# The front of a hybrid flow step: w_in as plain fp32 products, the S5 tables, splits and taps on VectorE alone, and the first modulation from row slabs

## The chip, the cores and the metric

The kernel runs on one core of one Trainium2 chip. The metric is the device time of one execution in microseconds; lower is better. TensorE is PE, VectorE DVE, ScalarE ACT, GpSimd POOL and SyncE SP in what follows.

## The reference, cut to what matters

One layer works on two groups of 128 tokens each (a context and a latent grid) with shared weights, D = 1024:

```python
mod = silu(cond) @ w_mod + b_mod            # per group; six parts of 1024: sh1, sc1, g1, sh2, sc2, g2
h = rmsnorm(x, norm1_g) * (1 + sc1) + sh1
z = h @ w_in + b_in                         # (256 tokens, 5120 columns)
z_f, z_a, z_b, z_s, z_g = split(z)          # 512 Fourier, 512 + 512 conv, 512 S5, 3 x 1024 gates
br_f = fft2(z_f).real @ w_four
br_c = silu(layernorm(depthwise_conv31(z_a * sigmoid(z_b)))) @ w_conv_out
y_s, finals = s5_bidirectional(z_s, ...)    # complex diagonal scan, 32 groups of 16 channels, 64 states
y_s = gelu(y_s) * sigmoid(gelu(y_s) @ w_ssm_glu + b)
br_s = y_s @ w_ssm_out
x = x + g1 * ((gate_f * br_f + gate_c * br_c + gate_s * br_s) @ w_out)
h = rmsnorm(x, norm2_g) * (1 + sc2) + sh2
x = x + g2 * moe(h)                         # 32 experts, top 4, clamped SwiGLU, d_ff 1024
return rmsnorm(x), finals
```

All is fp32. Weights are 1 MB slabs of fp32: 24 of w_mod, 20 of w_in, two for each of three branch projections, four of w_out, and then the experts'.

## The kernel before, in words

The program has a front (modulation, norm, w_in, the three branches, w_out, the router) and then the loop over the experts that tokens chose. The front is not written in engine order. Some thirty generators, one for each part of the work, yield operations; the class `Sched` plans them when the program is built: it keeps a planned time for every engine, adds a cost for each operation from the helpers (`tr` L262, `mm` L273, `ts` L279 and L282, `stt` L287, `tt` L291, `act` and `copy` L304, `vcopy` L311, `fill` L318), and takes next what can start earliest, weighted by the priorities in `PRIO`. So a changed cost or priority changes the order on every engine. On the chip each engine follows its own list, with semaphores between them.

Weights go through `Ring`: slabs are loaded over SP's queue in a fixed order into slots of 8 KB per partition, 23 in all, each as a slot falls free (`ring.done`, `ring.give`). The experts' slabs follow the front's in the same ring.

The parts that matter here:

- `first_mod` and `modulate` (L486 to L545): the first two parts of the modulation, 2048 columns, from eight slabs of w_mod. Before, a slab holds 256 columns of all 1024 rows, so four pieces become ready one after the other; each goes through a copy (`R0`), four transposes, a sum, an addition and a multiplication into `modA`, and then 4 of 16 blocks of the normed, transposed input `xT` are modulated.
- `splitter` and `main_products`: each slab of w_in, of a projection and of w_out is split into two fp32r parts, high (ACT copies 512 columns) and low (DVE or POOL subtracts); `faster` picks the engine by the planned times and the costs `CV`, `CG`. `prod3` then makes a product of three fp32r matmuls of 128x256. The modulated input is split the same way into `hhi` and `hlo`. `COLS` is the order of w_in's slabs ahead of the first projection: S5 columns (1536, 1792), Fourier columns (0, 256), then the conv's.
- S5: `s5_inputs` and `tables_in` make the input tables (four blocks, each of six 128x1024 operations in `cprod`), one generator on DVE and one on POOL, which share a list of blocks. `m1_transposes` turns them for PE. The scan is 16 steps of four 128x128 DVE operations. `tables_out` makes the output tables in the same way as `tables_in`. `kernel_table` makes the table Kd with small matmuls, writes it to DRAM and reads it back in another layout over SP's queue; the matmuls on it (called M3 here) and the S5 output gate follow.
- `taps_sum` makes the 31 taps of the conv for four blocks of 128 channels: three blocks as DVE operations of L287, the last (`NP` = 1) as ACT multiplications and POOL additions.
- `evacuate` takes w_in's and the projections' products out of PSUM and adds the gated branches (`mac`).

Of the kernel before, what the change touches and what calls it, by code (L numbers as in the profile page):

```python
# [205 lines left out]
def build(tc, A, O):  # L206
# [3 lines left out]
    with es:  # L210
# [216 lines left out]
        dma("Y", mrow[0:16], A["b_mod"][0, 0:2048].rearrange("(k p) -> k p", p=128))  # L427
        dma("Y", mrow[16:24], A["norm1_g"][0].rearrange("(k p) -> k p", p=128))
# [32 lines left out]
        R0 = [SL[15][:, 1024:1536], SL[15][:, 1536:2048]]  # L461
        modA = sm.tile([128, 2, 8, 2], F32, name="modA")
        pm = sm.tile([128, 4, 2], F32, name="pm")
        hhi = new(4, F32R)[:, :].rearrange("p (k t) -> p k t", k=8)
        hlo = new(5, F32R)[:, :].rearrange("p (k t) -> p k t", k=8)
# [31 lines left out]
        def first_mod():  # L497
# [19 lines left out]
        def modulate():  # L517

            for b in range(4):
                yield f"R{b}"  # L520
                if b == 0:
                    yield tr(PB[2][:, 64:96], mrow)
                    yield copy(vec[:, 60:84], PB[2][:, 64:88])
                for i in range(4):
                    yield tr(PB[2][:, i * 128:(i + 1) * 128], R0[b % 2][:, i * 128:(i + 1) * 128])
                flags.add(f"P{b}")
                k2 = slice(2 * b, 2 * b + 2)
                yield vsum(pm[:, :, :], PB[2][:, :].rearrange("p (i q r) -> p i r q", i=4, q=4)[:, :, 0:2])
                yield tt(modA[:, :, k2], pm[:, :, :].rearrange("p (s k) g -> p s k g", s=2), vec[:, 60:76].rearrange("p (s k) -> p s k", s=2)[:, :, k2, None].to_broadcast(
                    [128, 2, 2, 2]), OP.add)  # L530
                yield stt(modA[:, 1, k2], modA[:, 1, k2], 1.0, vec[:, 76 + 2 * b:78 + 2 * b, None].to_broadcast([128, 2, 2]),
                          op0=OP.add, op1=OP.mult)
# [8 lines left out]
                if b == 3:  # L541
                    yield tr(PB[2][:, 0:64], vrow)
                    yield copy(vec[:, 0:60], PB[2][:, 0:60])
                    flags.add("vec")
# [132 lines left out]
        def s5_inputs():  # L677
# [23 lines left out]
            yield tt(tb[2], Bt[:, 1], bch(fr), e="G")  # L701
            yield tt(tb[1], Bt[:, 1], bch(fi))
            yield tt(tb[3], Bt[:, 0], bch(fi), e="G")
            yield tt(Bb[:, 0], tb[0], tb[1], OP.subtract)
            yield tt(Bb[:, 1], tb[2], tb[3], OP.add, e="G")
# [59 lines left out]
        def faster(n, cv, cg):  # L765

            return "V" if sch.t["V"] + n * cv <= sch.t["G"] + n * cg else "G"
# [13 lines left out]
        Mtmp = [tbuf(SL16[:, 1024:2048]), tbuf(SL[11][:, 1024:2048])]  # L781

        def cprod(o_re, o_im, tmp, P, Q, Qi, j, e):
# [8 lines left out]
            yield tt(o_re, px(0), qx(Q[0]), e=e)  # L792
            yield tt(tmp, px(1), qx(Q[1]), e=e)
            yield tt(o_re, o_re, tmp, OP.subtract, e=e)
            yield tt(o_im, px(0), qx(Q[1] if Qi is None else Qi), e=e)
            yield tt(tmp, px(1), qx(Q[0]), e=e)
            yield tt(o_im, o_im, tmp, OP.add if Qi is None else OP.subtract, e=e)
# [5 lines left out]
        def tables_in(e, tmp, js):  # L803
            yield from need("Bb", "pw0")
            while js:
                j = js.pop(0)
                yield from cprod(*M1T[j], tmp, pw1, (Bb[:, 0], Bb[:, 1]), None, j, e)
                flags.add(f"T{j}")

        def m1_transposes(js, banks):  # L810
            yield from need("xT", "R2", *(("m0",) if js[0] else ()))
            for j in js:
                if j == 2:
                    yield "in0"
# [10 lines left out]
        def tables_out(e, tmp, js):  # L825
            yield from need("E", "columns", "pw1")
            while js:
                j = js.pop(0)
                yield from cprod(M2[j][:, :, 0], M2[j][:, :, 1], tmp, pw2, (Ct[:, 0], Ct[:, 1]), nCi, j, e)
# [50 lines left out]
        def s5():  # L880
# [100 lines left out]
            for o in range(4):  # L981
# [3 lines left out]
                yield from split(g2[:, c], m_[:, c], m_[:, 1024 + 256 * o:1280 + 256 * o], e="V")  # L985
# [3 lines left out]
        def taps_sum(j):  # L989
# [3 lines left out]
            for k in range(31):  # L993
                if j >= 4 - NP:
                    o = 1536 + 256 * (k % 2 if NP == 1 else j % 2)
                    o = av if k == 0 else SL17[:, o:o + 256].rearrange("p (b t) -> p b t", b=2)
# [4 lines left out]
                elif k == 0:  # L1001
# [5 lines left out]
        def conv():  # L1007
# [23 lines left out]
            for i in range(2):  # L1031
                c = slice(512 * i, 512 * i + 512)
                yield from split(HA[:, c], m_[:, c], m_[:, 1024 + 512 * i:1536 + 512 * i], e="V")
# [718 lines left out]
NP = 1  # L1752
# [22 lines left out]
```

## Time and profile before

| | us |
|---|---|
| median of 3 runs | 1414.85 (1414.38 to 1416.57) |
| profiled execution: its own time | 1418.22 |
| its span, first to last instruction | 1416.4 |
| PE busy (weight loads apart) | 1243.9 |
| DVE busy | 492.4 |
| ACT busy | 301.5 |
| POOL busy | 216.0 |
| mean granted PE clock | 0.961 |

The span is 1.8 us shorter than the execution's own time. The page's shares are averages over a front of some 385 us and an expert part of some 1015 us, which have different limits, so times have to be read by stage. The stages used below are cut at: the first S5 input table on DVE (29.4), the first w_in product (66.8), the first scan operation (107.1), the end of the scan (167.4), the start of Kd's writes (186.7), the first matmul on the Kd read back (219.8), the end of the S5 branch (255), the conv branch's first projection (317.5), the last w_out product (372.8), and the first expert matmul (385.1).

### The profile page before, as it was taken

The page shows a single profiled execution, that of the slowest core. Times are in us where ns is not written, and L with a number is a line of the kernel's source. Part 1 is how long each engine was busy: PE and PEld are TensorE (multiplying, and loading weights), DVE is VectorE, ACT ScalarE, POOL GpSimd, SP SyncE. Part 2 cuts the span into 40 slices and gives each one's busy share as a digit, 9 for nine tenths or more (in the row PEclk, how much of TensorE's full clock was granted, in tenths as well). Part 3 has the DMA queues.
Part 4 walks back from the last instruction along what each step waited for, and adds up shares of the span by engine and source line. Part 5 has one row for each costly group of instructions (what it writes and reads, how often), then busy time and mean ns, then how long its engine had stood idle before and what let it go on. Part 6 is the DMA issues. An engine that isn't in the chain of part 4 may idle for free. (4 is left out here: it accounts for less than half of the span.)

```text
span 1416.4 us, 19588 instructions
## 1 busy us (share of the span) xinstructions
PE 1243.9 (88%) x7444; PEld 655.7 (46%) x7444; DVE 492.4 (35%) x839; ACT 301.5 (21%) x609; POOL 216.0 (15%) x183
## 2 busy tenths in 40 slices
PE   4596787899999999999989999999999989999994
PEld 3475686789833433334343433333334334343331
DVE  7949898897511111111111111111121111211113
ACT  4454344454311101011100101101011101111011
POOL 4555556565300000000000000000000000000001
PEclk9798899999999999999999999999999999999996
DMA  9563489558799999999998999998999994999990
GB/s 268 193 210 115 144 146 266 188 196 316 290 352 410 416 397 415 416 416 415 417 415 319 407 417 414 415 400 357 416 416 416 416 409 185 413 415 415 414 395 33
DMA packets 124834, 477.08 MB, mean 337 GB/s; under 512 B 11871, under 2 KB 49505, under 8 KB 90864
## 3 DMA queue, kind: packets, MB, share of 16 engines
q1 hardware_dynamic: 121744, 468.25, 85.3%
q0 software_dynamic: 2288, 5.76, 1.2%
q8 instruction: 120, 1.97, 0.6%
q10 hardware_dynamic: 624, 0.63, 0.1%
q14 instruction: 58, 0.48, 0.1%
HBM read 472.61 MB, written 1.61 MB: 335 GB/s over the span
## 5 line engine op out<-in xcount | busy, mean ns | idle before, releaser
L273 PE MATMUL pb<-sl,sl 128*64 128x512 f32 (+4 forms) x5344 | 951.3, 485 | 48.7 <-PEq L1644 13.1
L273 PEld LDWEIGHTS pb<-sl,sl 128*64 128x64 f32 (+2 forms) x5344 | 438.4, 152 | 521.8 <-issue 445.2
L304 ACT ACTIVATE sl<-sl 128x512 fp32r<-128x512 f32 (+4 forms) x211 | 120.8, 588 | 614.2 <-DVE sl L279 496.4
L291 POOL TENSOR_TENSOR sl<-sl,sl 128x512 fp32r<-128x512 f32 (+4 forms) x73 | 121.1, 1667 | 737.5 <-DVE sl L291 607.7
L279 DVE TENSOR_SCALAR sl<-pb 128x512 f32<-128x512 f32 (+1 forms) x35 | 23.7, 676 | 434.7 <-PE pb L273 434.7
L287 DVE SCALAR_TENSOR_TENSOR sl<-pb,wsl,sl 128x512 fp32r<-128x512 f32 x64 | 47.7, 750 | 310.5 <-ACT sl L304 309.3
L291 DVE TENSOR_TENSOR sl<-sl,sl 128x512 fp32r<-128x512 f32 (+3 forms) x107 | 105.6, 1001 | 30.1 <-ACT sl L304 27.7
L304 ACT ACTIVATE sl<-pb 128x512 f32<-128x512 f32 (+6 forms) x125 | 68.5, 585 | 199.2 <-PE pb L273 177.8
L262 PE MATMUL pb<-cst,sl 128*128 128x128 f32 (+2 forms) x354 | 57.4, 296 | 46.0 <-ACT sl L304 15.0
L304 ACT ACTIVATE sl<-pb,wsl 128x512 fp32r<-128x512 f32 x64 | 43.6, 687 | 199.6 <-PE pb L273 196.6
L273 PE MATMUL pb<-sl,PT 128*128 128x512 f32 x256 | 78.0, 428 | 0.5 <-PEq L1644 0.5
L273 PE MATMUL pb<-hb,sl 128*128 128x128 f32 x512 | 68.4, 289 | 7.9 <-DVE hb L291 7.5
L273 PEld LDWEIGHTS pb<-hb,sl 128*128 128x128 f32 x512 | 65.1, 200 | 18.3 <-ACT wsl L304 11.8
L262 PEld LDWEIGHTS pb<-cst,sl 128*128 128x128 f32 (+2 forms) x354 | 43.7, 158 | 63.0 <-issue 26.1
L318 POOL MEMSET sl<- 128x30 f32 (+6 forms) x15 | 2.8, 228 | 374.1 <-PEq L1644 373.8
L287 DVE SCALAR_TENSOR_TENSOR hb<-sl,taps,hb 128x256 f32<-128x256 f32 x90 | 55.5, 664 | 0.6
L273 PEld LDWEIGHTS pb<-sl,PT 128*128 128x128 f32 x256 | 46.2, 201 | 8.0 <-ACT sl L304 1.3
L291 POOL TENSOR_TENSOR sl<-PWT,sl 128x1024 f32<-128x1024 f32 x20 | 43.5, 2190 | 11.1 <-PE pb L273 6.2
L273 PEld LDWEIGHTS pb<-comb,hb 128*128 128x128 f32 x128 | 19.6, 207 | 44.6 <-DVE sl L279 41.9
L291 DVE TENSOR_TENSOR sl<-sl 128x512 f32<-128x512 f32 (+4 forms) x77 | 37.1, 500 | 4.1 <-ACT sl L304 0.5
L273 PE MATMUL pb<-comb,hb 128*128 128x1 f32 x128 | 22.0, 241 | 18.2 <-PEq L1644 16.4
L273 PE MATMUL pb<-ha,selb 128*64 128x512 bf16 (+1 forms) x140 | 21.3, 390 | 16.8 <-PEq L1644 14.4
(176 smaller groups left out, 547.0 us busy)
## 6 DMA issues: line engine op xcount, KB each, us to landing
sl<-w_gate_up SPq DMA_DIRECT2D x256, 1024.0 KB, 14.9
sl<-w_down SPq DMA_DIRECT2D x128, 1024.0 KB, 17.5
sl<-w_mod SPq DMA_DIRECT2D x24, 1024.0 KB, 7.2
sl<-w_in SPq DMA_DIRECT2D x20, 1024.0 KB, 11.1
sl<-w_out SPq DMA_DIRECT2D x4, 1024.0 KB, 6.9
sl<-md POOLq DMA_DIRECT2D x6, 512.0 KB, 6.9
sl<-w_four SPq DMA_DIRECT2D x2, 1024.0 KB
sl<-Kd SPq DMA_DIRECT2D x16, 128.0 KB, 9.2
```

Of the source, the lines that this page charges most:

```text
L262: return sch.op("P", 0.107 * in_.shape[0] / 128, [out], [in_], lambda: te.transpose(out, in_, ident[:in_.shape[0], :in_.shape[0]]))
L273: lambda: te.matmul(out, lhsT, rhs, start=start, stop=stop, skip_group_check=True))
L279: return sch.op(e, c, [o], ap, lambda: ENG[e].tensor_scalar(o, a, s1, None, op0=op0))
L287: lambda: ENG[e].scalar_tensor_tensor(o, a, sc, b, op0=op0, op1=op1))
L291: return sch.op(e, c, [o], [a, b], lambda: ENG[e].tensor_tensor(o, a, b, op=op))
L304: [a] + [x for x in (bias, scale) if hasattr(x, "tensor")], lambda: s.activation(o, a, func, **kw))
L318: return sch.op(e, size(o) * 0.9e-3 + 0.1, [o], [], lambda: ENG[e].memset(o, val))
```

## The change

- w_in's products are plain fp32: 16 matmuls of 128x256 per slab on the slab as loaded and on `xT`, which `modulate` overwrites in place (ACT for one group, DVE for the other). Only the projections' and w_out's slabs are split, all by ACT and DVE. `hhi`, `hlo`, `UNITS`, `faster`, `CV` and `CG` go.
- POOL makes no tables, no splits, no tap additions and no additions of gated branches; all four tap blocks and both kinds of table are on DVE.
- The first modulation reads eight slabs of 128 whole rows, 2048 columns each; `adaln`, the function for the later slabs, makes four 32x512 matmuls of each, and `modA` is made once for all.
- The biases of the modulation and the norm's gain are loaded over POOL's queue instead of SP's, the S5 input matrices over ACT's. All first slots are given at once.
- `COLS` has the Fourier columns first. The gated sums lie in slot 5 instead of 20, and those slots are given back at other points. The planner's cost of an fp32r matmul is 4.6e-4 us per column instead of 4.17e-4.

```diff
@@ mm
-                c = max(n, m) * 4.17e-4
+                c = max(n, m) * 4.6e-4
@@ ring
-        for k in range(4):
-            if k == 3:
-                add_cols(("in", COLS[0]), A["w_in"][0], COLS[0], 256, 8)
-            for i in range(2):
-                add_cols(("m0", k, i), A["w_mod"][0], 1024 * i + 256 * k, 256, 8)
+        for k in range(8):
+            ring.add(("m0", k), lambda sl: sl[:, :], A["w_mod"][0, k * 128:(k + 1) * 128, 0:2048])
+        add_cols(("in", COLS[0]), A["w_in"][0], COLS[0], 256, 8)
@@ loads
-        dma("Y", mrow[0:16], A["b_mod"][0, 0:2048].rearrange("(k p) -> k p", p=128))
-        dma("Y", mrow[16:24], A["norm1_g"][0].rearrange("(k p) -> k p", p=128))
-            dma("Y", BR[i].rearrange("g d p h -> g d (p h)"), A[n][0].rearrange("d g p h -> g d (p h)"))
-        start(0, 1)
-        start(2, 3)
-        start(6, 7, 8, 9)
+            dma("S", BR[i].rearrange("g d p h -> g d (p h)"), A[n][0].rearrange("d g p h -> g d (p h)"))
+        start(0, 1, 2, 3, 6, 7, 8, 9, 4)
+        dma("G", mrow[0:16], A["b_mod"][0, 0:2048].rearrange("(k p) -> k p", p=128))
+        dma("G", mrow[16:24], A["norm1_g"][0].rearrange("(k p) -> k p", p=128))
@@ first_mod
-            for b in range(4):
-                for i in range(2):
-                    w = ring.get(("m0", b, i))[:, :].rearrange("p (k c) -> p k c", k=8)
-                    for k in range(8):
-                        q = 32 * (k % 4)
-                        yield mm(PB[b % 2][q:q + 32, 256 * i:256 * i + 256], cs[:, k, :], w[:, k], k < 4 and i == 0, k >= 4)
-                    ring.done(("m0", b, i))
-                if b > 1:
-                    yield f"P{b - 2}"
-                yield copy(R0[b % 2], PB[b % 2][:, :])
-                flags.add(f"R{b}")
+            for k in range(8):
+                yield from adaln(("m0", k), PB[0])
+                if k == 4:
+                    flags.add("R0")
@@ modulate
+            yield "m0"
+            yield copy(R0, PB[0][:, :])
+            for i in range(4):
+                yield tr(PB[2][:, i * 128:(i + 1) * 128], R0[:, i * 128:(i + 1) * 128])
...
             for b in range(4):
-                yield f"R{b}"
...
                 yield f"xT{b}"
                 for k in (2 * b, 2 * b + 1):
                     for g in range(2):
-                        yield act(hhi[:, k, 128 * g:128 * g + 128], xT[:, k, g], AF.Identity, bias=modA[:, 0, k, g:g + 1],
-                                  scale=modA[:, 1, k, g:g + 1])
-                        yield ts(xT[:, k, g], xT[:, k, g], modA[:, 1, k, g:g + 1], modA[:, 0, k, g:g + 1])
-                    yield tt(hlo[:, k], flat(xT[:, k]), fv(hhi[:, k]), OP.subtract)
+                        if g:
+                            yield ts(xT[:, k, g], xT[:, k, g], modA[:, 1, k, g:g + 1], modA[:, 0, k, g:g + 1])
+                        else:
+                            yield act(xT[:, k, g], xT[:, k, g], AF.Identity, bias=modA[:, 0, k, g:g + 1], scale=modA[:, 1, k, g:g + 1])
@@ split
-        def split(src, hi, lo, e=None):
+        def split(src, hi, lo):
             yield copy(hi, src)
-            yield tt(lo, src, fv(hi), OP.subtract, e=e or faster(size(src), CV, CG))
+            yield tt(lo, src, fv(hi), OP.subtract)
@@ taps_sum
-                if j >= 4 - NP:
...
-                    yield act(o, vp[:, j, :, k:k + 128], AF.Identity, scale=taps[:, j, k:k + 1],
-                              **({"bias": vec[:, 40 + j:41 + j]} if k == 0 else {}))
-                    if k:
-                        yield tt(av, av, o, OP.add, e="G")
@@ main_products
+                if key[0] == "in":
...
+                    for n, (k, c) in enumerate((x, c) for x in range(8) for c in range(2)):
+                        if key == seq[0] and c == 0:
+                            yield f"hmod{k}"
+                        yield mm(bk[:, c * 256:(c + 1) * 256], w[:, k, c * 128:(c + 1) * 128], flat(xT[:, k]), n == 0, k == 7)
@@ generators
-                         ("in", tables_in("V", Mtmp[0], js[0])), ("in", tables_in("G", Mtmp[1], js[0])),
+                         ("in", tables_in(Mtmp)),
-                         ("out", tables_out("V", Mtmp[0], js[1])), ("out", tables_out("G", Mtmp[1], js[1])),
+                         ("out", tables_out(Mtmp)),
@@ constants
-COLS = (1536, 1792, 0, 256, 1024, 1280, 512, 768)
+COLS = (0, 256, 1536, 1792, 1024, 1280, 512, 768)
```

The order of the instructions moves on every engine. On DVE, the end of the scan before (`sl_847` is the scan's state, `A8r` and `A8i` its factors, `sl_396<-..,sl_395` a low part of w_in, `PWT` a table product, `sl_1116` a low part of the Fourier branch):

```order
L291 TENSOR_TENSOR sl_847<-sl_847,w_156 128x128
L291 TENSOR_TENSOR sl_396<-sl_69,sl_395 128x512
L291 TENSOR_TENSOR sl_847<-sl_847,w_156 128x128
L291 TENSOR_TENSOR sl_74<-sl_74,sl_84 128x8x128
L291 TENSOR_TENSOR sl_74<-PWT,sl_80 128x8x128
L291 TENSOR_TENSOR sl_84<-PWT,sl_80 128x1024
L291 TENSOR_TENSOR w_156<-A8i,sl_847 128x128
L291 TENSOR_TENSOR w_156<-A8r,sl_847 128x128
L291 TENSOR_TENSOR sl_396<-sl_70,sl_395 128x512
L291 TENSOR_TENSOR sl_847<-sl_847,w_156 128x128 x2
```

and the same place in the change (`sl_754` is the scan's state, `fin` its end, `sl_85` the conv's input vp):

```order
L291 TENSOR_TENSOR w_154<-A8i,sl_754 128x128
L291 TENSOR_TENSOR w_154<-A8r,sl_754 128x128
L291 TENSOR_TENSOR sl_754<-sl_754,w_154 128x128 x2
L311 COPY fin<-sl_754 128x8x4 x2
L291 TENSOR_TENSOR sl_74<-sl_74,sl_84 128x8x128
L291 TENSOR_TENSOR sl_74<-PWT,sl_80 128x8x128
L291 TENSOR_TENSOR sl_84<-PWT,sl_80 128x1024
L287 SCALAR_TENSOR_TENSOR sl_85<-pb_93,vec,ha 128x2x128 x2
L291 TENSOR_TENSOR sl_74<-sl_74,sl_84 128x8x128
L291 TENSOR_TENSOR sl_75<-PWT,sl_80 128x8x128
```

The scan's steps stand next to each other now, and the output tables behind them, all of them on DVE.

On DVE at the start of the change (`sl_79` holds the input factors, `cs` the condition, `sl_87` is `xT`):

```order
L291 TENSOR_TENSOR cs<-pb_95,csg 128x2x8
L291 TENSOR_TENSOR sl_85<-PWT,sl_79 128x1024
...
L291 TENSOR_TENSOR sl_84<-sl_84 128x1024
L291 TENSOR_TENSOR sl_78<-PWT,sl_79 128x1024
L291 TENSOR_TENSOR modA<-pb_95,vec 128x16
L287 SCALAR_TENSOR_TENSOR modA<-modA,vec 128x16
L291 TENSOR_TENSOR modA<-pb_95,vec 128x16
L282 TENSOR_SCALAR sl_87<-sl_87,modA 128x128 x6
```

Twelve table operations stand between `cs` and the three for `modA`; before, four sets of small `modA` operations were spread over the tables.

On PE, the first product of w_in before (`sl_147` and `sl_148` are the parts of a slab, `sl_395` and `sl_396` those of the input):

```order
L273 MATMUL pb_94<-sl_68,cs 32x256 x8
L262 MATMUL pb_96<-cst,sl_83 128x128
L262 MATMUL pb_96<-cst,sl_84 128x128
L262 MATMUL pb_95<-cst,sl_83 128x128 x4
...
L273 MATMUL pb_93<-sl_147,sl_395 128x256
L273 MATMUL pb_93<-sl_148,sl_395 128x256
L273 MATMUL pb_93<-sl_147,sl_396 128x256
```

and in the change (`sl_72` is the slab itself):

```order
L273 MATMUL pb_93<-sl_76,cs 32x512 x4
L477 MATMUL pb_100<-ones 64x64
L273 MATMUL pb_93<-sl_77,cs 32x512 x4
L262 MATMUL pb_96<-cst,sl_85 128x128 x4
...
L262 MATMUL pb_98<-cst,sl_85 128x128 x4
L273 MATMUL pb_93<-sl_87,sl_72 128x256 x4
L273 MATMUL pb_95<-sl_68,cs 32x512 x4
```

The eight w_mod slabs stand ahead of all transposes of tables but a few, and one matmul stands where three did.

## Rows read from the trace of the kernel before

**Rows 1.** Stages: bounds, length, busy of PE, PEld, DVE, ACT, POOL, clock, DMA share, GB/s.

```profile
29.40:66.70 37.30, 23.05 (x185) 13.54 (x186) 36.71 (x43) 17.15 (x39) 25.88 (x19) 0.82 0.73 240
...
107.10:167.40 60.30, 37.51 (x245) 31.91 (x244) 58.09 (x80) 26.49 (x59) 38.06 (x19) 0.79 0.31 109
...
255.00:317.50 62.50, 55.49 (x432) 53.64 (x433) 55.53 (x74) 30.75 (x57) 39.11 (x37) 0.95 0.51 171
317.50:372.80 55.30, 52.87 (x417) 51.31 (x416) 35.34 (x42) 26.12 (x55) 29.34 (x26) 0.97 0.84 312
...
385.10:1400.00 1014.90, 937.83 (x4718) 387.97 (x4717) 164.23 (x278) 120.86 (x239) 3.11 (x6) 0.98 0.96 388
```

**Rows 2.** Timeline of DVE: start, length, engine, line, operation, count [idle before <-what ended it].

```profile
58.57 2.72 DVE L291 TENSOR_TENSOR sl<-sl,sl 128x512 fp32r<-128x512 f32 x1
...
61.48 1.22 DVE L291 TENSOR_TENSOR sl<-PWT,sl 128x1024 f32<-128x1024 f32 x1
...
107.31 0.68 DVE L291 TENSOR_TENSOR sl<-sl,sl 128x512 fp32r<-128x512 f32 x1
...
111.59 0.29 DVE L291 TENSOR_TENSOR w<-A8i,sl 128x128 f32<-128x128 f32 x1
...
112.65 0.29 DVE L291 TENSOR_TENSOR w<-A8i,sl 128x128 f32<-128x128 f32 x1
...
123.29 4.42 DVE L291 TENSOR_TENSOR sl<-sl,w 128x128 f32<-128x128 f32 x2
...
216.98 2.45 DVE L287 SCALAR_TENSOR_TENSOR hb<-sl,taps,hb 128x256 f32<-128x256 f32 x6
```

**Rows 3.** Timeline of POOL beside the first of them.

```profile
58.34 2.40 POOL L291 TENSOR_TENSOR sl<-sl,sl 128x1024 f32<-128x1024 f32 x1
```

**Rows 4.** DVE's groups, 0 to 385.1: line, operation, shapes, count, busy, mean ns, idle before.

```profile
L291 DVE TENSOR_TENSOR sl<-sl,sl 128x512 fp32r<-128x512 f32 x74 | 74.9, 1022 | 26.0 <-ACT sl L304 25.5
L287 DVE SCALAR_TENSOR_TENSOR hb<-sl,taps,hb 128x256 f32<-128x256 f32 x90 | 55.5, 664 | 0.6
L291 DVE TENSOR_TENSOR sl<-sl,w 128x128 f32<-128x128 f32 x32 | 23.4, 730 | 0.4
L291 DVE TENSOR_TENSOR sl<-PWT,sl 128x1024 f32<-128x1024 f32 x12 | 19.5, 1647 | 5.4 <-PE pb L273 5.4
```

**Rows 5.** PE windows: fp32 and fp32r products (busy, clock, DMA); one timeline row.

```profile
238.19:245.20 7.01, 7.01 (x33) 1.00 1.08 362
172.29:179.18 6.89, 6.89 (x60) 1.00 1.03 361
...
103.51 6.97 PE L273 MATMUL pb<-sl,sl 128*128 128x256 f32 x56
```

**Rows 6.** Timeline of PE and ACT: first w_in product, S5 columns out, kernel table, its reader.

```profile
66.79 3.12 PE L273 MATMUL pb<-sl,sl 128*128 128x256 f32 x13
...
89.53 0.84 ACT L304 ACTIVATE sl<-pb,vec 128x256 f32<-128x256 f32 x2 [0.48 <-PE pb L273]
...
179.65 0.40 PE L273 MATMUL pb<-sl,sl 128*32 128x16 f32 x5
...
219.82 0.64 PE L273 MATMUL pb<-sl,sl 128*32 128x128 f32 x4 [5.28 <-DMA sl<-Kd]
```

**Rows 7.** Timeline of SP's queue.

```profile
6.24 19.65 SPq L256 DMA_DIRECT2D sl<-w_mod  x6
...
186.71 9.55 SPq L256 DMA_DIRECT2D Kd<-sl  x16
...
324.81 24.50 SPq L256 DMA_DIRECT2D sl<-w_gate_up  x8
```

**Rows 8.** List of waits, 0 to 385.1: total us, times, longest.

```profile
PE pb L273 <- ACT sl L304: 17.5, 7, 11.9
PE pb L273 <- DVE sl L291: 10.3, 6, 3.8
PE pb L273 <- POOL sl L291: 7.8, 6, 4.4
```

More of the change, by code (lines that the diff above doesn't have):

```diff
@@ L460, in build @@
         xT = SL[20][:, :].rearrange("p (k g t) -> p k g t", k=8, g=2)
[L461 removed]
+        R0 = SL[15][:, 1024:1536]
         modA = sm.tile([128, 2, 8, 2], F32, name="modA")
[L463 to L465 removed]
         def adaln(key, bk):
@@ L801, in need, with tables_in @@
                 yield x
-        def tables_in(e, tmp, js):
+        def tables_in(tmp):
             yield from need("Bb", "pw0")
-            while js:
-                j = js.pop(0)
-                yield from cprod(*M1T[j], tmp, pw1, (Bb[:, 0], Bb[:, 1]), None, j, e)
+            for j in range(4):
+                yield from cprod(*M1T[j], tmp, pw1, (Bb[:, 0], Bb[:, 1]), None, j)
                 flags.add(f"T{j}")
         def m1_transposes(js, banks):
-            yield from need("xT", "R2", *(("m0",) if js[0] else ()))
+            yield from need("xT", "m0")
             for j in js:
-                if j == 2:
-                    yield "in0"
                 yield f"T{j}"
@@ L823, in m1_transposes, with tables_out @@
                 flags.add(f"M1{j}")
-        def tables_out(e, tmp, js):
+        def tables_out(tmp):
             yield from need("E", "columns", "pw1")
-            while js:
-                j = js.pop(0)
-                yield from cprod(M2[j][:, :, 0], M2[j][:, :, 1], tmp, pw2, (Ct[:, 0], Ct[:, 1]), nCi, j, e)
+            for j in range(4):
+                yield from cprod(M2[j][:, :, 0], M2[j][:, :, 1], tmp, pw2, (Ct[:, 0], Ct[:, 1]), nCi, j)
                 flags.add(f"M2{j}")
@@ L984, in s5 @@
                 yield tt(g2[:, c], g1[:, c], g2[:, c])
-                yield from split(g2[:, c], m_[:, c], m_[:, 1024 + 256 * o:1280 + 256 * o], e="V")
+                yield from split(g2[:, c], m_[:, c], m_[:, 1024 + 256 * o:1280 + 256 * o])
             mixhi[2], mixlo[2] = j4(m_[:, 0:1024]), j4(m_[:, 1024:2048])
@@ L1032, in conv @@
                 c = slice(512 * i, 512 * i + 512)
-                yield from split(HA[:, c], m_[:, c], m_[:, 1024 + 512 * i:1536 + 512 * i], e="V")
+                yield from split(HA[:, c], m_[:, c], m_[:, 1024 + 512 * i:1536 + 512 * i])
             mixhi[1], mixlo[1] = j4(m_[:, 0:1024]), j4(m_[:, 1024:2048])
@@ L1052, in fourier @@
                 c = slice(512 * i, 512 * i + 512)
-                yield from split(PB[6 + i][:, :], m_[:, c], m_[:, 1024 + 512 * i:1536 + 512 * i], e="V")
+                yield from split(PB[6 + i][:, :], m_[:, c], m_[:, 1024 + 512 * i:1536 + 512 * i])
             mixhi[0], mixlo[0] = j4(m_[:, 0:1024]), j4(m_[:, 1024:2048])
@@ L1068, in splitter @@
             n = 0
-            for key in seq + [("out", q) for q in range(4)]:
-                for u in UNITS if key == seq[0] else range(4):
+            for key in [x for x in seq if x[0] == "pr"] + [("out", q) for q in range(4)]:
+                for u in range(4):
                     yield lambda: key in ring.ready and cnt["used"] >= n - NW + 1
@@ L1110, in main_products @@
                     yield f"mix{i}"
-                for u in UNITS if key == seq[0] else range(4):
-                    if key[0] == "in":
-                        c, first, last = u // 2, u == 0, u % 2 == 1
-                        K, xh, xl = range(4 * (u % 2), 4 * (u % 2) + 4), hhi, hlo
-                    else:
-                        c, first, last = u % 2, u % 2 == 0, True
-                        K, xh, xl = range(4), mixhi[i], mixlo[i]
-                    if first:
+                if key[0] == "in":
+                    bk = PB[cnt["bank"] % 2]
+                    yield from bank()
+                    yield lambda: key in ring.ready
+                    w = ring.get(key)[:, :].rearrange("p (k c) -> p k c", k=8)
+                    for n, (k, c) in enumerate((x, c) for x in range(8) for c in range(2)):
+                        if key == seq[0] and c == 0:
+                            yield f"hmod{k}"
+                        yield mm(bk[:, c * 256:(c + 1) * 256], w[:, k, c * 128:(c + 1) * 128], flat(xT[:, k]), n == 0, k == 7)
+                    ring.done(key)
+                    evac.append((key[1], bk))
+                    if key == ("in", seq[-2][1]):
+                        ring.give(20)
+                    continue
+                for u in range(4):
+                    c = u % 2
+                    if c == 0:
                         bk = PB[cnt["bank"] % 2]
@@ L1122, in main_products @@
                     hi, lo = spl.pop((key, u))
-                    for n, k in enumerate(K):
-                        if key == seq[0]:
-                            yield f"hmod{k}"
-                        yield from prod3(bk[:, c * 256:(c + 1) * 256], hi[:, n], lo[:, n], xh[:, k], xl[:, k], first and n == 0,
-                                         last and n == 3)
+                    for k in range(4):
+                        yield from prod3(bk[:, c * 256:(c + 1) * 256], hi[:, k], lo[:, k], mixhi[i][:, k], mixlo[i][:, k],
+                                         c == 0 and k == 0, k == 3)
                     cnt["used"] += 1
-                    if key[0] == "in" and u == 3:
-                        evac.append((key[1], bk))
-                    elif key[0] == "pr" and c == 1:
+                    if c == 1:
                         evac.append((key, u // 2, bk))
-                if key == ("in", seq[-2][1]):
-                    new(4)
-                    new(5)
-                    ring.give(4, 5)
             for q in range(4):
@@ L1175, in evacuate @@
                             if h and q:
-                                ring.give(20)
+                                ring.give(5)
                 elif isinstance(job[0], tuple):
```

72 lines of the change are left out of this document (27 added, 45 removed).

## The prediction

> **What bounds the kernel now.** I read the table by stage first [rows 1]. The experts, from 385.1 to 1400, move 388 GB/s with the DMA engines 96% busy; nothing in the change touches them, so its effect has to be found in the 385 us ahead of them. There TensorE (PE) works only in part: busy 23.1 of 37.3 us before the first w_in product and 37.5 of 60.3 in the stage of the S5 scan, but 108.4 of 117.8 in the last two stages before the router. VectorE (DVE) looks full where PE is not: 36.7 of 37.3 and 58.1 of 60.3 us.
>
> Then the DVE rows, to see whether that busy time is work [rows 2]. One scan step is four 128x128 operations and takes 1.06 us, from 111.59 to 112.65; at 123.29 two of its adds alone take 4.42. Six conv taps take 2.45 us at 216.98, 0.41 each; their mean is 0.664 [rows 4]. A table product of 128x1024 takes 1.22 us at 61.48, the mean is 1.647. A split takes 0.68 at 107.31 and 2.72 at 58.57. Same shapes, same operands: the long ones contain a wait inside the instruction. Its cause shows at 58.34, where GpSimd (POOL) starts a 128x1024 addition of 2.40 us [rows 3]: the DVE split that begins at 58.57 ends 0.55 us after POOL does, about as long as it takes alone. So a POOL tensor operation holds DVE up, and the grouped rows give the price [rows 4]: splits 74 x (1.022 - 0.69) = 24.6 us, taps 90 x (0.664 - 0.41) = 22.9, scan updates 32 x (0.730 - 0.29) = 14.1, table products 12 x (1.647 - 1.22) = 5.1. In four rows that is 67 us of DVE time that does no work.
>
> **The change, part by part.**
>
> *PE.* 320 products of w_in go from three fp32r matmuls to one fp32 matmul each. The S5 output gate shows what fp32 costs: 16 products of 128x256 leave 33 records in 7.01 us (two a matmul, and one of the next kind), 0.431 us each. Of fp32r, one dense stretch has 60 records in 6.89 us, 0.115 each, and one 56 in 6.97, 0.124 [rows 5]; I take 0.12, 0.36 a product. So +0.071 x 320 = **+22.7 us** of PE (27 and 19 by the two ends). A rule of the Trainium skill weighs on this: "FP8 and Floating Point Precision", section TensorE Precision Notes, counts true fp32 as four passes. With three fp32r matmuls as three such passes of 0.107, a product would go from 0.32 to 0.43: an estimate of +34 us by that page. The rows decide for 22.7, since an fp32r matmul takes longer here than a quarter of an fp32 one.
>
> *DVE and POOL.* 20 table products and some ten additions of 128x1024 come to DVE: 30 x 1.22 = 36.6 us; 31 taps x 0.41 = 12.7; small ones 2. From DVE go 28 splits (net of those it takes over), 28 x 0.69 = 19.3, eight narrow subtracts and eight modulations, 5.8, and the piecewise modulation, 1.5. Net **+24 us** of work, against 67 us or more of waits that go. POOL keeps memsets, DMAs and a few late additions. ScalarE loses 80 copies of 128x512 and the 30 tap scalings; it waits for others nearly everywhere, so I count nothing.
>
> *Start.* The first product stands at 66.79 [rows 6]. Before it, four pieces need transposes, a reduction and small DVE steps each, caught between tables and POOL. Now w_mod's eight row slabs are read first. Six such issues took 19.65 us [rows 7], so eight take 26, and with landing they are there by about 33. DVE runs twelve table operations, then the three of modA: from about 27 (29.4 before, with POOL in the way) + 12 x 1.2 = 41. First product at **42.5**. But two Fourier slabs now stand ahead of the S5 columns. To the end of the second S5 slab PE has 4 x 16 x 0.431 = 27.6 us of products, and five modulation slabs, 62 transposes and the Fourier matmuls, some 20: 90 if it never waits, 95 with 5 for waits. From the evacuation of the S5 columns at 89.53 [rows 6] to the scan at 107.1 it took 17.6; so the scan starts at **113**, 6 later; bounds 105 and 122.
>
> *Scan and tables.* 16 steps at 1.06 are 17 us in place of 60.3: the scan ends at 130. What was woven into it now stands behind: 22 table operations x 1.17 = 25.7, four additions into vp 1.9, eight splits 5.2, taps and gates 4, kernel inputs 1.8, together 39. The kernel table's matmuls can start at **169**; they started 12 after the scan's end before, at 179.65 [rows 6]. PE has six slabs, one projection and the scan's inputs to do in 117 to 169, 53 us, so it is just full too. Gain: 10.
>
> *Round trip.* The kernel table goes to DRAM and back over SP's queue as before: 33 us from the start of its writes at 186.71 [rows 7] to the matmuls that wait for it at 219.82 [rows 6], which come at **210**. From there to the end of the S5 branch it was 35.2 us; with splits and taps at their short durations I take 30: 240, gain **15**.
>
> *Last stretch.* 117.8 us now, from 255 to 372.8. Since PE took up w_in 24 us earlier, less is left behind the S5 branch: in the new order six w_in slabs (96 x 0.431 = 41.4), four projections (192 x 0.12 = 23) and w_out (23), 88 with few transposes. The conv branch must be there for its projection at 240 + 39 = 279; 120 taps x 0.41 = 49 and its norm, in the gaps of S5's work, bring it at about 282 (317.5 before). With 10 for handoffs and for matmuls after an idle, when the granted clock falls (0.79 in the scan stage [rows 1]), 98: gain **20** more. Sum **-35**. The experts then start at 350 instead of 385.1 and take the same time, as their loads go by slots that w_in, the projections and w_out set free, all earlier.
>
> *At nothing:* the modulation's bias and the norm's gain on POOL's DMA queue (needed at 39, and POOL has no tensor work ahead; were they late, modA and all behind it would be late by as much); ssm_b on ScalarE's queue, where little stands; the gate sums in another slot.
>
> The profiled run took 1418.2 us (span 1416.4), 3.4 above the median of 1414.85. On its own basis 1383; against the median **1380**. Differences under 0.2%, 2.8 us, are about what a measurement of this kernel cannot tell from none.
>
> **Rivals.**
> 1. *PE was the limit anyhow (slower).* In the list of waits PE waits 10.3 us for DVE and 7.8 for POOL, but 17.5 for ScalarE alone [rows 8]. If its idle time is set by evacuations, the round trip and the order, and stays, then +22.7 stands in full: 1415 + 23 = 1438. It decides once less than 23 us of the front's idle PE time goes. Against it: 23 us idle in the scan stage, beside a DVE that POOL holds up, and 24 us at the start. Chance 0.12.
> 2. *DVE's long durations are its own.* Then the scan stays near 60 us, DVE takes 24 more, the kernel table starts at about 200, and with the 5 us that PE cannot hide, 1415 + 25 = 1440. Against it: the ends that meet at 60.7 [rows 2, 3]. Chance 0.03.
> 3. *The experts' loads do not move (same).* Their first eight slabs are issued at 324.81 [rows 7], 60 us before the first expert, and 388 GB/s leave nothing to catch up; if the slots come free no earlier, the end stays within 3 us, 1415. Little speaks for it: the slots are those of w_in and the projections. Chance 0.05.
> 4. *More falls away.* If the S5 columns come at 88 and the scan at 106, and the last stretch takes 91, -35 - 7 - 7 and some of the 10 in the round trip: -55, 1360. Chance 0.18.
>
> **How the numbers follow.** My forecast with its bounds (scan start 105 to 122, last stretch 91 to 108) spans 1365 to 1402 and has 0.62. The range takes in most of rival 4 and leaves 1 to 3 outside: 1357 to 1402. Faster: 0.62 + 0.18, 0.80; same 0.05; slower 0.15.
>
> **What would show it.** Right: first 128x256 product near 42; a scan of 17 to 20 us; no table product over 1.3 us; POOL busy under 40 us instead of 216; kernel table at 169, its reader at 210, conv's projection at 282, experts from 350; 6.9 us for an fp32 slab. Wrong: PE idle for over 50 us between 42 and 330; fp32 products over 0.45 us; a scan that starts after 125; or slabs of w_in that come too late for a PE that takes them from 42 on.

## The result, and the profile after

The changed kernel takes 1380.38 us in the median of 4 runs (1379.95 to 1380.85), the kernel before on the same chip 1414.62 (1413.87 to 1416.57): a ratio of 0.9756, with a 95% interval of 0.9739 to 0.9773. The prediction was 1380.0.

The stages of the changed kernel, cut at the same events as before [rows 1]: first table operation after the condition (26.8), first w_in product (45.2), scan (111.4 to 128.5), start of the kernel table's writes (174.6), its reader (207.3), first of the products behind the S5 branch (234.8), conv's first projection (281.0), last w_out product (338.8), first expert matmul (351.2). Columns: bounds, length, then busy time (records) of PE, PEld, DVE, ACT, POOL, the granted clock, DMA share and GB/s.

```profile
26.80:45.20 18.40, 17.05 (x103) 6.55 (x103) 16.25 (x19) 8.43 (x20) 0.86 (x8) 1.00 1.01 373
45.20:111.40 66.20, 63.05 (x404) 44.13 (x405) 21.65 (x29) 25.53 (x52) 0.00 (x0) 1.00 0.60 194
111.40:128.50 17.10, 17.10 (x91) 14.35 (x91) 15.97 (x67) 13.09 (x32) 0.00 (x0) 1.00 0.55 184
128.50:174.60 46.10, 45.56 (x491) 38.20 (x490) 44.36 (x68) 8.56 (x19) 0.00 (x0) 1.00 0.66 229
174.60:207.30 32.70, 19.98 (x224) 17.93 (x222) 22.91 (x57) 2.07 (x6) 6.61 (x10) 0.87 0.94 101
207.30:234.80 27.50, 26.30 (x172) 22.74 (x172) 20.58 (x49) 10.48 (x22) 0.00 (x0) 0.91 0.89 297
234.80:281.00 46.20, 41.68 (x242) 36.57 (x242) 36.70 (x73) 12.23 (x23) 9.61 (x15) 1.00 0.80 277
281.00:338.80 57.80, 56.80 (x388) 53.62 (x388) 31.42 (x45) 21.03 (x44) 8.60 (x7) 0.94 0.51 196
351.20:1362.00 1010.80, 937.83 (x4720) 387.05 (x4719) 164.36 (x279) 121.10 (x239) 3.12 (x6) 0.99 0.96 390
```

PE is now nearly full at the full clock from 45.2 to 174.6 (63.1 of 66.2, 17.1 of 17.1, 45.6 of 46.1 us), where it stood idle for 23 us in the scan stage alone before, at 0.79 of its clock [rows 1]. Over the whole front PE was busy 303.9 of 385.1 us and is now busy 310.0 of 351.2: its idle time falls by 40 us and its work grows by 6. The front is 33.9 us shorter (385.1 to 351.2), and the experts take 4.1 less. One hole is left, 12.7 us of 32.7 while the kernel table is on its way.

DVE's groups in 0 to 350 (operation, shapes, count, busy us, mean ns of one, idle before), against [rows 4]:

```profile
L287 DVE SCALAR_TENSOR_TENSOR hb<-sl,taps,hb 128x256 f32<-128x256 f32 x120 | 50.8, 477 | 0.4
L291 DVE TENSOR_TENSOR sl<-PWT,sl 128x1024 f32<-128x1024 f32 x32 | 38.0, 1218 | 20.2 <-PE pb L273 20.1
L291 DVE TENSOR_TENSOR sl<-sl,sl 128x512 fp32r<-128x512 f32 x44 | 31.6, 747 | 19.0 <-ACT sl L304 18.5
L291 DVE TENSOR_TENSOR sl<-sl,w 128x128 f32<-128x128 f32 x32 | 9.2, 288 | 0.6
```

The same operations as before at 1.218 us instead of 1.647 (table product), 0.288 instead of 0.730 (scan update), 0.477 instead of 0.664 (tap), 0.747 instead of 1.022 (split). DVE does 20 table products and 30 taps more, 30 splits fewer, and is less busy: 415.7 us of the span instead of 492.4.

Three rows of PE's timeline (start, length, operation, count of records, idle before and what ended it) mark the first product, a dense stretch of fp32 products in the scan, and the kernel table's reader:

```profile
45.20 2.00 PE L273 MATMUL pb<-sl,sl 128*128 128x256 f32 x8 [0.78 <-ACT sl L304]
...
110.46 12.79 PE L273 MATMUL pb<-sl,sl 128*128 128x256 f32 x58
...
207.32 5.40 PE L273 MATMUL pb<-sl,sl 128*32 128x128 f32 x66 [12.74 <-DMA sl<-Kd]
```

29 products in 12.79 us are 0.441 each, where 0.431 was taken [rows 5].

### The profile page after: what moved, and what is told of

It reads as the page before. It is cut to its first block, busy times and chain, and to the rows that moved or that the text cites. A ratio compares the mean times of both kernels' runs of the same rounds, so it can differ in the third digit from the quotient of the medians.

```text
span 1378.4 us, 18435 instructions
## 1 busy us (share of the span) xinstructions
PE 1249.9 (91%) x7070; PEld 642.5 (47%) x7070; DVE 415.7 (30%) x849; ACT 239.6 (17%) x487; POOL 43.4 (3%) x71
## 3 DMA queue, kind: packets, MB, share of 16 engines
q10 hardware_dynamic: 784, 1.16, 0.3%
## 5 line engine op out<-in xcount | busy, mean ns | idle before, releaser
L273 PE MATMUL pb<-sl,sl 128*64 128x512 f32 (+5 forms) x5024 | 960.9, 507 | 36.8 <-PEq L1609 14.0
L273 PEld LDWEIGHTS pb<-sl,sl 128*64 128x64 f32 (+2 forms) x5024 | 430.5, 147 | 522.5 <-issue 438.0
L304 ACT ACTIVATE sl<-sl 128x512 fp32r<-128x512 f32 (+5 forms) x131 | 72.5, 564 | 557.1 <-DVE sl L279 494.8
L262 PE MATMUL pb<-cst,sl 128*128 128x128 f32 (+2 forms) x342 | 52.4, 285 | 29.9 <-DVE sl L279 10.6
L273 PEld LDWEIGHTS pb<-hb,sl 128*128 128x128 f32 x512 | 66.5, 204 | 18.0 <-ACT wsl L304 12.7
L291 DVE TENSOR_TENSOR sl<-sl,sl 128x512 fp32r<-128x512 f32 (+3 forms) x80 | 65.4, 841 | 19.9 <-ACT sl L304 18.5
L262 PEld LDWEIGHTS pb<-cst,sl 128*128 128x128 f32 (+2 forms) x342 | 39.8, 152 | 49.5 <-issue 13.6
L287 DVE SCALAR_TENSOR_TENSOR hb<-sl,taps,hb 128x256 f32<-128x256 f32 x120 | 50.8, 477 | 0.4
L291 DVE TENSOR_TENSOR sl<-PWT,sl 128x1024 f32<-128x1024 f32 x32 | 38.0, 1218 | 20.2 <-PE pb L273 20.1
L291 POOL TENSOR_TENSOR sl<-sl,sl 128x512 f32<-128x512 f32 (+3 forms) x11 | 16.4, 1505 | 651.3 <-DVE sl L291 636.4
L273 PE MATMUL pb<-sl,cs 128*32 128x512 f32 (+1 forms) x256 | 29.5, 508 | 0.6 <-PEq L1609 0.5
## 6 DMA issues: line engine op xcount, KB each, us to landing
sl<-w_down SPq DMA_DIRECT2D x128, 1024.0 KB, 17.1
```

The lines of the kernel that those rows point to most:

```text
L262: return sch.op("P", 0.107 * in_.shape[0] / 128, [out], [in_], lambda: te.transpose(out, in_, ident[:in_.shape[0], :in_.shape[0]]))
L287: lambda: ENG[e].scalar_tensor_tensor(o, a, sc, b, op0=op0, op1=op1))
L291: return sch.op(e, c, [o], [a, b], lambda: ENG[e].tensor_tensor(o, a, b, op=op))
L304: [a] + [x for x in (bias, scale) if hasattr(x, "tensor")], lambda: s.activation(o, a, func, **kw))
```

## The experiments

Theory A says that a POOL tensor operation holds DVE up, and that the gain comes from taking the two apart. The rivals give it to the earlier start (B), to nothing that POOL does (C), or let PE's added work set the end (D); E to G are about single parts. All ratios are against the kernel before, timed beside each.

**e1: POOL off, w_in still in pairs.**

```diff
-            return "V" if sch.t["V"] + n * cv <= sch.t["G"] + n * cg else "G"
+            return "V"
-NP = 1
+NP = 0
-                         ("in", tables_in("V", Mtmp[0], js[0])), ("in", tables_in("G", Mtmp[1], js[0])),
+                         ("in", tables_in("V", Mtmp[0], js[0])),
```

The output tables and three operations on the S5 inputs are moved in the same way.

> The kernel before with POOL's tables, splits and taps on DVE, w_in still in pairs. Theory A (a POOL tensor operation holds DVE up): DVE takes over 50 splits x 0.69, 31 table operations x 1.22 and 31 taps x 0.41, 85 us of work, and loses the 67 us or more of waiting; the scan falls from 60 us to under 35, and the kernel comes to 1395 to 1412. Rival B (the gain is from the earlier start and the fp32 products, POOL only helped): DVE is overloaded by 85 us, 1420 to 1450. Rival C (DVE's long durations are its own): the scan stays at 55 us or more.

Measured: 1421.46 us, ratio 1.0033 [1.0007, 1.0059]. The scan fell to 34.2 us, as theory A has it, and the first product came at 45.2; but the time did not fall. 1421 lies in rival B's range (DVE overloaded), not in theory A's: what DVE's added work costs was underrated. In the stage between the scan and the table's writes DVE is busy 54.3 of 58.3 us, with splits between the table operations, and PE then waits 28.3 us for the table with nothing else in its list:

```profile
110.30:144.50 34.20, 34.20 (x306) 32.05 (x305) 30.13 (x91) 27.93 (x60) 0.00 (x0) 1.00 0.70 238
144.50:202.80 58.30, 44.81 (x573) 42.94 (x571) 54.34 (x82) 21.06 (x40) 0.00 (x0) 0.88 0.50 169
202.80:235.10 32.30, 3.78 (x129) 3.50 (x128) 23.66 (x61) 0.43 (x3) 6.34 (x10) 0.59 0.95 102
```

The group of splits in the whole front is the largest of its DVE rows:

```profile
L291 DVE TENSOR_TENSOR sl<-sl,sl 128x512 fp32r<-128x512 f32 x124 | 85.5, 704 | 30.9 <-ACT sl L304 29.6 <-issue 0.3
```

Each split is fast, 0.704 us, but all 124 are DVE's. 21 of them take 14.5 us of the scan's 34.2, and 26 take 17.9 us of the next stage, beside 26.8 of table operations. The change has 44 splits in all. The ACT copies that go with the splits are there too, and no run takes the two apart.

**e2: w_in in fp32, POOL still on tables, taps and the splits that are left.** The splitter leaves w_in out, and its products are made as in the change:

```diff
-            for key in seq + [("out", q) for q in range(4)]:
+            for key in [x for x in seq if x[0] == "pr"] + [("out", q) for q in range(4)]:
+                if key[0] == "in":
...
+                        yield mm(bk[:, c * 256:(c + 1) * 256], w[:, k, c * 128:(c + 1) * 128], flat(xT[:, k]), n == 0, k == 7)
```

> The kernel before with w_in as plain fp32 products, POOL still on tables, on the splits that are left and on taps. Theory A: PE takes 22.7 us more, but 80 splits less on ACT, DVE and POOL make most waits shorter; POOL's tables still lengthen DVE's operations, a mean table product of DVE stays over 1.4 us; 1395 to 1420. Rival D (PE is the limit through and through): 1433 to 1440.

Measured: 1420.38 us, ratio 1.0027 [1.0014, 1.004], just above the upper edge of what theory A gave. It is not rival D's 1433 to 1440: PE's added 22.7 us do not appear in full. But the tables still run beside POOL:

```profile
L291 DVE TENSOR_TENSOR sl<-PWT,sl 128x1024 f32<-128x1024 f32 x16 | 28.0, 1784 | 10.6 <-PE pb L273 10.6
```

1.784 us for a table product; the scan takes 42 us (105.7 to 147.7), the first product stands at 59.5.

**e3: both edits, with the old column slabs and the old order of columns.**

> Both edits, without the row slabs and with the S5 columns first. Theory A: no DVE table product over 1.3 us, scan 17 to 20 us, first product at about 60 instead of 66.8; 1385 to 1400, so most of the 34 us are here. Rival B (the earlier start makes most of it): 1405 to 1415.

Measured: 1369.7 us, ratio 0.9656 [0.9634, 0.9678], faster than the whole change, and below both theory A's 1385 to 1400 and rival B's 1405 to 1415. Each of the two edits alone costs 0.3%, both together gain 3.4%. The first product stands at 44.3, where about 60 was expected, and the scan runs from 86.1 to 110.3, 24 us for the 17 to 20 expected:

```profile
0.00:44.30 44.30, 29.14 (x256) 19.26 (x256) 33.27 (x139) 21.27 (x40) 5.41 (x24) 1.00 0.98 306
44.30:86.10 41.80, 40.57 (x284) 26.77 (x281) 25.20 (x32) 18.57 (x38) 0.00 (x0) 1.00 0.63 209
86.10:110.30 24.20, 24.20 (x133) 19.38 (x132) 21.45 (x71) 17.65 (x40) 0.00 (x0) 1.00 0.54 182
```

So the early start is not the row slabs' doing. The rows of DVE in this kernel show the pieces of the old modulation slipping between table operations, the first at 36 us:

```profile
29.98 2.35 DVE L291 TENSOR_TENSOR sl<-PWT,sl 128x1024 f32<-128x1024 f32 x2
35.81 0.19 DVE L315 TENSOR_REDUCE pm<-pb 128x8 f32<-128x32 f32 x1 [3.48 <-PE pb L262]
36.04 0.17 DVE L291 TENSOR_TENSOR modA<-pm,vec 128x8 f32<-128x8 f32 x1
36.24 0.16 DVE L287 SCALAR_TENSOR_TENSOR modA<-modA,vec 128x4 f32<-128x4 f32 x1
```

**e4: the change with the S5 columns first.** `COLS = (1536, 1792, 0, 256, 1024, 1280, 512, 768)`.

> The changed kernel with the old order of columns, S5 before Fourier. Theory A: the scan starts 14 us earlier (near 97), but PE is nearly full from 45 to 339, so the end moves little: 1375 to 1385. Rival E (the column order is where the gain is from): 1390 or more.

Measured: 1375.95 us, ratio 0.9713 [0.9697, 0.9729]. Within what theory A gave, though the scan starts at 92.2 rather than 97, 19 us earlier than in the change. The new order of columns therefore loses some 4 us by the medians and 6 by the ratios.

**e5: the change with POOL back on half of the tables, on splits and on a block of taps.**

> The changed kernel with POOL back on half of the tables, on the splits that are left and on the fourth block of taps, all else as changed. Theory A: DVE's table products go back to a mean of 1.5 us or more, the scan to 25 us or more; 1388 to 1410. Rival B (POOL's share makes no difference): within 3 us of 1380.

Measured: 1437.72 us, ratio 1.0172 [1.0145, 1.0199], more than theory A's 1388 to 1410 and above the kernel before. The first product stands at 63.7 and the scan takes 40.7 us.

**f3: of these, POOL's half of the tables alone.**

```diff
-                         ("in", tables_in(Mtmp)),
+                         ("in", tables_in("V", Mtmp, JS[0])), ("in", tables_in("G", Mtmp1, JS[0])),
-                         ("out", tables_out(Mtmp)),
+                         ("out", tables_out("V", Mtmp, JS[1])), ("out", tables_out("G", Mtmp1, JS[1])),
```

> The changed kernel with POOL back on half of the tables alone. Of the 57 us between the change and e5 this tells the part of the tables. Theory A: a POOL table operation of 2 us costs DVE about as much as the two save together, so DVE's mean table product goes over 1.6 us and the end comes 5 to 40 us later: 1385 to 1420. Rival B: POOL's half of the tables is free work, 1375 to 1381.

Measured: 1415.61 us, ratio 0.9995 [0.9976, 1.0014]. The tables on two engines take back the whole gain, 34 us by the ratios, though the planner also moves other operations when these move. The first product stands at 64.1, and the scan, with the output tables beside it, takes 46 us. The timelines of the two engines (DVE, then POOL) show what happens at the input tables:

```profile
33.99 6.25 DVE L291 TENSOR_TENSOR sl<-PWT,sl 128x1024 f32<-128x1024 f32 x2
40.28 2.83 DVE L291 TENSOR_TENSOR sl<-sl,sl 128x1024 f32<-128x1024 f32 x1
43.04 6.23 DVE L291 TENSOR_TENSOR sl<-PWT,sl 128x1024 f32<-128x1024 f32 x2
...
36.26 5.78 POOL L291 TENSOR_TENSOR sl<-PWT,sl 128x1024 f32<-128x1024 f32 x2
42.11 3.21 POOL L291 TENSOR_TENSOR sl<-sl,sl 128x1024 f32<-128x1024 f32 x1
45.29 5.76 POOL L291 TENSOR_TENSOR sl<-PWT,sl 128x1024 f32<-128x1024 f32 x2
```

From 33.99 to 43.04 DVE gets through three operations, and POOL through three from 36.26 to 45.29: six in 9.05 us, 1.51 each. DVE alone needs 1.22, or 1.18 by its pace in the change. The equal pace of the two looks as if they took turns, POOL's being the longer: 3.02 us for one of each, of which DVE's part alone would be 1.22.

**e6 and e7: useless work on POOL during the scan.** On 512 columns that nothing else uses, started by a small fill after the first scan step. The lists of PE, ACT and SP and the rest of DVE's are those of the change.

```diff
+        def extra():
+            yield "scr"
+            for _ in range(20):
+                yield tt(scr[:, :], scr[:, :], scr[:, :], OP.add, e="G")
```

> The changed kernel with 20 additions of 128x512 on POOL, 1.4 us each, on data that nothing else uses, from the first scan step on; the lists of PE, ACT and SP are unchanged, DVE's has one small fill more. Theory A: the scan goes from 17 us to 35 to 45 though it waits for nothing new, and as the kernel table stands behind it the time rises to 1388 to 1400. Rival C (no hold): scan 17, 1380.

> The same place with 50 memsets of 128x512 on POOL, 25 to 30 us together, in place of the additions. If only POOL operations that read two tensors hold DVE up: scan 17 to 18 us and 1380. If any POOL write to SBUF does: as with the additions, scan 30 us or more.

Measured: with the additions 1394.08 us, ratio 0.9854 [0.983, 0.9877]; with the memsets 1381.29, 0.9771 [0.9746, 0.9797], which is that of the change. The timelines of e6 (POOL's extra work, and one scan step of DVE during it and one after it):

```profile
114.47 23.20 POOL L291 TENSOR_TENSOR sl<-sl 128x512 f32<-128x512 f32 x20 [69.49 <-DVE sl L318]
...
120.44 1.08 DVE L291 TENSOR_TENSOR w<-A8i,sl 128x128 f32<-128x128 f32 x1
121.44 0.28 DVE L291 TENSOR_TENSOR w<-A8r,sl 128x128 f32<-128x128 f32 x1
121.65 2.24 DVE L291 TENSOR_TENSOR sl<-sl,w 128x128 f32<-128x128 f32 x2
...
139.96 0.29 DVE L291 TENSOR_TENSOR w<-A8i,sl 128x128 f32<-128x128 f32 x1
140.17 0.28 DVE L291 TENSOR_TENSOR w<-A8r,sl 128x128 f32<-128x128 f32 x1
140.37 0.61 DVE L291 TENSOR_TENSOR sl<-sl,w 128x128 f32<-128x128 f32 x2
```

A scan step takes 3.48 us (120.44 to 123.92) while POOL adds, and 1.06 as soon as it has finished at 137.7. An addition takes 23.20 / 20 = 1.16 us, so a step is as long as three of them, which fits engines that take turns. The scan goes from 17 to 33 us, a little less than expected (35 to 45), and the 16 us come back as 14 in the time. The 50 memsets of e7 fill the same place and leave a step as it is:

```profile
113.97 29.04 POOL L318 MEMSET sl<- 128x512 f32 x50 [69.53 <-DVE sl L318]
...
116.19 0.28 DVE L291 TENSOR_TENSOR w<-A8r,sl 128x128 f32<-128x128 f32 x1
116.39 0.61 DVE L291 TENSOR_TENSOR sl<-sl,w 128x128 f32<-128x128 f32 x2
```

**f1: e4 with the first modulation from column slabs again,** in four pieces, all else as in e4.

> The changed kernel with S5 columns first (e4: 1376) and with the first modulation from column slabs, in pieces, as before. Theory A (with POOL off, the pieces' small operations find DVE free between table operations, so the first product comes as early as with row slabs, and modulation and tables share the wait for w_mod): scan near 86, 1366 to 1372, so the row slabs cost 4 to 10 us. Rival F (the 6 us between e3 and e4 come from the other edits: queues, slots, planner's cost): 1374 to 1379.

Measured: 1373.82 us, ratio 0.9707 [0.9674, 0.9741], the same as e4 within the intervals. The median is just below rival F's range (1374 to 1379) and outside theory A's (1366 to 1372); the scan starts at 90.2 and not near 86. So the row slabs neither cost nor gain what can be measured here. The step from e3 (0.9656) to e4 and f1 is then in the other edits (the queues of small loads, the slots given, the planner's cost of an fp32r matmul); which of them was not tried. The intervals of e3 and e4 lie apart, those of e3 and f1 just touch, so the step is small and its cause open.

**f2: e3 with the Fourier columns first.**

> The kernel of e3 (w_in in fp32, POOL off, nothing else; 1370) with the Fourier columns first. As the S5 branch then waits for two more slabs, 13.8 us, and PE has the same work, theory A has the scan start 12 to 18 us later, near 100, the wait of PE for the kernel table unchanged and the time 3 to 7 us longer: 1372 to 1378. Rival G (order does not matter, as PE is full): 1369 to 1371.

Measured: 1375.51 us, ratio 0.971 [0.9678, 0.9741], against e3's 0.9656. The scan starts at 108.8 instead of 86.1, later than expected (near 100), and PE's wait for the kernel table stays, at 15.6 us. The time is within theory A's range, though the two intervals touch. With e4 this is the second time that the new order of columns comes out slower, by some 4 to 6 us in the medians (6 to 8 by the ratios).

**e8 and f4: the hole at the kernel table.** The planner counts the table's reads at four times their cost, and puts whole w_in slabs ahead of the table's reader.

```diff
+            if src.tensor.name[:2] == "Kd":
+                n *= KDF
+KDF = 4
```

> The changed kernel with a planner that counts the reads of the kernel table at four times the cost, which is nearer to the 33 us that the trip takes: PE's list has two whole w_in slabs (32 products) ahead of M3 instead of 3 products. If the slabs are there in time, the 12.7 us for which PE waits for the table fall to under 3 and the time to 1368 to 1375. If the slabs come over SP's queue behind the table's own reads, PE waits for them instead, and it is 1378 to 1386.

> The kernel of e3 with a planner that counts the kernel table's reads at four times the cost. e3 has PE wait 13.5 us for the table, e8 gained 2 to 4 us from this edit. The gap falls to under 5 us, the time to 1360 to 1368; if PE then waits for slabs or for the conv branch instead, 1369 to 1372.

Measured: e8 1378.63 us, ratio 0.976 [0.9732, 0.9788], no gain against the change (0.9756), so the gain of 2 to 4 us that f4's expectation counts on is not shown; f4 1373.12, 0.9683 [0.9652, 0.9713], none against e3 and above both ranges given for it. e8's time is in the range that was given for slabs that come too late, but not for that reason. In e8 the hole is filled and comes back at the next place, where PE waits for the S5 branch (PE's timeline):

```profile
174.37 32.70 PE L275 MATMUL pb<-sl,sl 128*128 128x256 f32 x282
207.56 2.37 PE L275 MATMUL pb<-sl,sl 128*32 128x128 f32 x64 [0.50 <-DMA sl<-Kd]
210.62 1.09 PE L264 MATMUL pb<-cst,sl 128*128 128x128 f32 x8 [0.69 <-ACT sl L306]
222.34 9.17 PE L275 MATMUL pb<-sl,sl 128*128 128x256 f32 x32 [10.63 <-DVE sl L293]
```

PE waits 0.5 us at the table instead of 12.7, and 10.6 behind it, where the change has 20.3 us of products without a wait (from 213.44): the work that filled one hole was, by its place in the lists, the work that had covered the other. In f4 the wait for the table stayed at 13.3 us, so there the edit did not do what it says.

## Why the prediction was right, step by step

**The clock of events.** Predicted and measured: first product 42.5 and 45.2; scan start 113 and 111.5; scan 17 and 17 (111.4 to 128.5); the kernel table's reader 210 and 207.3; conv's projection 282 and 281.0; experts 350 and 351.2. The sum was -35, the medians differ by 34.2. Part of the closeness is luck. The kernel table's matmuls started at 172.6, not 169, but its writes followed 2 us behind them where they took 7 before, and the S5 branch ended at 234.8, 5 us ahead of the 240 taken. The last stretch then took 104.0 us, not 98: PE's work in it was 98.5 us where 88 was added up, and its idle time 5.5 where 10 was allowed. The two errors cancel. The experts were to take the same time; between the two profiled runs, which differ by 38.0 us, they take 4.1 less, and as the profiled run before was 3.6 above the median of 1414.62, no run here shows whether that is a gain.

**The hold, 67 us of DVE time.** Its cause is right, and shown for the scan: e6 brings it back with work that no one waits for, on the same lists, while DVE's list of waits stays empty. The means of [rows 4] fell to within 0.07 us of the base durations taken from single rows. But 67 us was too much. A tap was taken at 0.41 us, the pace of a run of taps, while a mean is the length of one instruction, and each starts a little before the one ahead of it has ended. The kernel of e1, without POOL, has both: a pace of 0.40 in this row, and a mean of 0.474.

```profile
196.44 8.00 DVE L287 SCALAR_TENSOR_TENSOR hb<-sl,taps,hb 128x256 f32<-128x256 f32 x20
```

With the change's own means as the base, the four groups of [rows 4] lost 56 us. "Rival 2" (DVE's long durations are its own) is refuted by e6, though its "ends that meet at 60.7" do not meet: POOL's addition ends at 60.74, DVE's split at 61.29 [rows 2, 3]. The Trainium skill's "SBUF — State Buffer", section "Who interferes with whom", describes a port pair that DVE and GpSimd share under an exclusive lock; e6 agrees (a step of 1.06 us takes 3.48 under POOL's additions), and e7's memsets, which hold nothing up, agree with a hold that depends on POOL's kind of operation.

**PE's +22.7 us.** The row held: 0.441 us a product in the change against 0.431 taken, 3 us more over 320 products. As busy time the whole of it does not appear: 1472 records of 128x256 took 204.0 us before and 1152 take 214.9 now, 10.9 more, at a mean granted clock of 0.97 in the front instead of 0.91. The estimate of +34 us by the Trainium skill's "FP8 and Floating Point Precision", section "TensorE Precision Notes", has no support in these rows: it needs fp32r matmuls at 0.107 us, and the dense stretches of before give 0.115 to 0.124 [rows 5].

**"Rival 1", PE the limit anyhow,** fell: it was to decide if less than 23 us of PE's idle time in the front went, and 40 went; in e2 only 0.3% was lost. But it named the right budget. In e3 PE is busy 155.7 of 157.3 us behind the table, so a further gain there has to come from PE's own work; the wait of 13.5 us for the table stands ahead of it. "Rival 3" fell too: the experts start 33.9 us earlier and take no longer. "Rival 4" wanted the scan at 106 and a last stretch of 91; they came at 111.5 and 104. Of the signs, POOL's busy time missed by a little, 43.4 us where under 40 was named.

**The step that failed: "Start".** The prediction gave the 24 us at the start mainly to "w_mod's eight row slabs" that are "read first", with POOL in the way as a side matter. e1 and e3 read the old column slabs and have their first product at 45.2 and 44.3; e5 and f3 read row slabs, with POOL on the tables, and have it at 63.7 and 64.1. It is POOL's half of the input tables, beside DVE's, that made the first product late; f1, with column slabs and a first product at 45.7, shows no price either way for the slabs. The rows of DVE at `modA`, in the change and in f3:

```profile
44.09 0.17 DVE L291 TENSOR_TENSOR modA<-pb,vec 128x16 f32<-128x16 f32 x1 [1.94 <-PE pb L262]
...
61.06 0.16 DVE L291 TENSOR_TENSOR modA<-pb,vec 128x16 f32<-128x16 f32 x1
```

In the change thirteen table operations (not the twelve counted) stand ahead of it, from 26.80 to 42.14, 1.18 us each, and then it waits 1.9 us for PE's transposes; in f3 twelve stand there, from 27.11 to 61.06, 2.83 us each. The size was right because the sum took the table operations at 1.2 us each, which they reach without POOL; the cause that was named was not.

**"6 later" for the S5 columns** was counted as neutral in the end, since PE is full. e4 and f2 price it: some 4 to 6 us of loss in the medians. From the start of its writes to its reader the table takes 31.6 to 36.5 us in every run, wherever it starts, so a later scan would move that wait to where less work is left to put in front of it. That reason is argued from e8, not shown.

**What the prediction did not see:** that the two main edits only pay together. Without fp32 products DVE has 124 splits (85.5 us) in and around the scan and the tables (e1); with POOL still on the tables, DVE's table products take 1.784 us and its scan 42 (e2). The prediction priced the edits as one sum and got the sum right, though each of the two main ones alone is worth +0.3% and the pair without the rest -3.4%, more than the whole change.

The best version that was run is e3, 1369.7 us, 0.9656 of the kernel before; the changed kernel is 0.9756.

## What to carry to other kernels

Where two engines seem to share elementwise work, compare the mean duration of a shape with its shortest row before adding the engines' speeds: here both together made a table operation in 1.51 us and one alone in 1.22. A long duration in a row can be a wait that no list of waits shows; and where short operations overlap, the pace of a run of them, and not the mean duration, is what one costs. And an edit that moves work to an engine is worth what is left of that engine: try it together with the edit that frees it, and price the small parts of a change apart, since two of this one's four did not pay: the row slabs made no difference that could be measured, and the order of columns lost.

## What the runs showed of the hardware

POOL additions of 128x512, 23.2 us in all, lengthened a DVE scan on other data by 16 us; memsets of the same shape for 29 us did not. DVE and POOL, both on table operations, made one in 1.51 us between them, slower than DVE alone at 1.22. DVE's taps of 128x256 followed one another at 0.40 us while each lasted 0.47. Filling the hole of 12.7 us in PE's list moved it by one stage and gained nothing.
